# Three PSUM banks at a retention chunk's start, ten background steps to a chunk, five pumps in a pair

## The chip, the cores and the metric

The kernel runs on one core of a Trainium2 chip. The metric is the device time of one execution in microseconds (us); the time before is the median of 3 runs.

## The reference, cut to what matters

One layer of a decoder is computed for 512 prompt positions and 64 sample positions together (576 columns, kept as two halves of 288). A combined projection feeds three branches: retention, window attention and a short convolution. Each branch is projected, gated and summed; an output projection, a feed-forward network and a per-layer embedding gate follow. The retention branch works in chunks of 128 positions with a state that passes from chunk to chunk:

```python
def step(s, inp):
    qi, ki, vi = inp
    inner = jnp.einsum('bhid,bhjd->bhij', qi, ki) * dmask
    o = jnp.einsum('bhij,bhje->bhie', inner, vi) + jnp.einsum('bhid,bhde->bhie', qi * q_dec, s)
    s = s * c_dec + jnp.einsum('bhjd,bhje->bhde', ki * k_dec, vi)
    return s, o
...
o = o * lax.rsqrt(jnp.mean(o * o, axis=-1, keepdims=True) + EPS)
return jax.nn.silu(rg) * o, s
```

## The kernel before

**Matrix products.** Weights are 128x128 tiles. Every fp32 weight and activation is split into a high and a low part, and three matmuls (high-high, high-low, low-high) stand for one. `product` (L329) is twelve matmuls of 288 columns into one PSUM bank: four tiles times three parts. `pair` multiplies a 2x2 block matrix by a Strassen-like scheme in seven such products, issued in this order: b11 (bank `pa`), t3 (`pe`), t2 (`pbb`), b21 (`pa`), t1 (`pbb`), t4 (`pe`), b22 (`pbb`). Between them ScalarE copies banks (L390, L396, L400), and `done` hands out a finished quarter. In `value`, VectorE forms c22 from `pbb` (L426) after t1, and b22 then adds to that same bank; it forms c21 from `pe` (L424) after t4. `unit` (L501) is a plain product of 24 matmuls for the branch projections.

**Weights.** `step()` advances a generator that loads raw weights through SP's DMA queue, adds blocks on VectorE (L227), casts the high part on ScalarE (L256) and subtracts for the low part on VectorE (L257). Four high and four low buffers hold what is ready.

**Background work.** `pump()` runs one step of a generator, up to its next `yield`. Before, a `pair` has four pumps: after t3, after the c11 hand-out that follows b21, after t4, and at its end. Each `unit` of a branch projection has one. `ret_gen` is the first background generator. A chunk's first step transposes v (bank `pv`, L708), multiplies k by q (banks `pst[0]`, `pst[1]`, L713; each head pair uses columns 0 to 255), masks both on VectorE (L717) and transposes k into a fourth bank `pk` (L721), which VectorE scales (L723). The third step makes the chunk's output `po` (L737, L739). The fifth updates the state (L744, L751) and enters `ret_out`: ScalarE squares `po` (L681). The seventh sums the squares on TensorE (`pn`, L685) and runs `rsqrt`: VectorE transposes and adds (L548, L554), POOL raises to a power (L555), VectorE finishes (L556, L557, L560, L562), then multiplies `po` by the gate (L690) and by the result (L691). An eighth empty step follows. Called below "the chain": L685 to L691.

The conv stage is six pairs, the gate stages are four times a pair and two units, and three pairs make the attention inputs. `ret_gen` runs four chunks and then the sample part (L763 onward) across the conv stage, the conv gates and the attention inputs. `att_gen` runs under the four retention gates; `drain()` finishes what is left of it before the attention gates.

**Banks and order.** The pool `psum` has six banks, shared by `pa`, `pe`, all background banks and most unit banks; `psb` has two, for `pbb`. A tile framework sets buffers, waits and the order of each engine's instructions ahead of time; on the chip each engine works through its list in that order. The order is not strictly the program's: an instruction of a later step may stand ahead of an earlier one.

Of the kernel before, what the change touches and what calls it, by code (L numbers as in the profile page):

```python
# [84 lines left out]
def decoder_step(ctx: ExitStack, tc: tile.TileContext, xT, pT, W, consts, smalls, s0q, s0t, ckT, cv,  # L85
# [25 lines left out]
    def nm(s):  # L111
        uid[0] += 1
        return f"{s}{uid[0]}"
# [7 lines left out]
    def bgtile(dt=F32):  # L121
        return bgt.tile([P, 512], dt, tag="bgt", name=nm("bgt"))

    def bank(s="ps"):
        return psum.tile([P, 512], F32, tag="ps", name=nm(s))

    def seeded(s="pbb"):
        return psb.tile([P, 512], F32, tag="ps", name=nm(s))
# [7 lines left out]
    def halft():  # L136
        return hlf.tile([P, H], F32, tag="hlf", name=nm("hlf"))
# [158 lines left out]
    def step(n=1):  # L296
        for _ in range(n):
            next(make, None)
# [17 lines left out]
    def nextpair():  # L316
        j, kind = items[pos[0]]
        assert kind != "one"
        need(j, "t2")
        pos[0] += 1  # L320
        return made.pop(j).w

    def product(bank, w, x, start):

        (hi, lo), s = w
        for j in range(4):
            xh, xl = x(j)
            for i, (lhs, rhs) in enumerate(((hi, xh), (hi, xl), (lo, xh))):
                PE.matmul(bank[:, :H], lhsT=lhs[:, s + j, :], rhs=rhs, start=start and j == 0 and i == 0,  # L329
                          stop=j == 3 and i == 2, skip_group_check=True)  # L330
# [52 lines left out]
    def pair(X, done, first=False, **kw):  # L383


        q = Job()
        q.w, q.t = nextpair(), {}
        q.a, q.b, q.e = bank("pa"), seeded(), bank("pe")
        product(q.a, q.w["b11"], X("a11"), True)
        A.activation(q.b[:, :H], q.a[:, :H], AF.Copy, scale=-1.0)  # L390
        if first:
            product(q.a, q.w["b21"], X("a12"), False)
            done(q, "c11")
        product(q.e, q.w["t3"], X("s3"), True)
        q.es = halft()
        A.copy(out=q.es, in_=q.e[:, :H])  # L396
        step()
        pump()
        product(q.b, q.w["t2"], X("s2"), False)
        A.copy(out=q.e[:, :H], in_=q.b[:, :H])  # L400
        if not first:
            product(q.a, q.w["b21"], X("a12"), False)
            done(q, "c11")
        step()
        pump()
        product(q.b, q.w["t1"], X("s1"), False)
        done(q, "c22")
        product(q.e, q.w["t4"], X("a22"), False)
        done(q, "c21")
        step()  # L410
        pump()
        product(q.b, q.w["b22"], X("x3"), False)
        done(q, "c12")
        step()
        pump()
# [64 lines left out]
    def pump(n=1):  # L480
        for _ in range(n):
            while bg:
                try:
                    next(bg[0])
                    break
                except StopIteration:
                    bg.pop(0)
# [184 lines left out]
    for t in (0, 2):  # L672
        pair(ops, gate_r(t), t == 0)
# [3 lines left out]
    def ret_out(po, w, c0):  # L677

        ov = po[:, :4 * w]
        sq = bgtile()  # L680
        A.activation(sq[:, :4 * w], ov, AF.Square)  # L681
        yield
        yield
        pn = bank("pb")
        PE.matmul(pn[:, :4 * w], lhsT=ones_h, rhs=sq[:, :4 * w], start=True, stop=True)  # L685
        rs = bgtile()
        rsqrt(pn[:, :4 * w], 4 * w, rs[:, :4 * w], 0.5)
        t1 = bgtile()
        t1v = t1[:, :4 * w].rearrange("p (h i) -> p h i", h=4)
        V.tensor_tensor(out=t1v, in0=ov.rearrange("p (h i) -> p h i", h=4), in1=rg[:, :, c0:c0 + w], op=ALU.mult)  # L690
        V.tensor_tensor(out=ro[:, :, c0:c0 + w], in0=t1v,  # L691
                        in1=rs[:, :4 * w].rearrange("p (h i) -> p h i", h=4), op=ALU.mult)

    def hrow(h):
        return slice(64 * (h % 2), 64 * (h % 2) + 64)

    def odd(a, q):

        return a.rearrange("p (t q i) -> p t q i", t=2, q=2)[:, :, q, :]

    def ret_gen():
        vt = big.tile([P, 4, T], F32, tag="big", name="vt")
        state = None
        for c in range(4):
            cs = slice(128 * c, 128 * c + 128)
            pv = bank("pb")
            for h in range(4):
                PE.transpose(pv[:, 128 * h:128 * h + 128], rv[:, h, cs], ident)  # L708
            vc = vt[:, c, :512]
            A.copy(out=vc, in_=pv)  # L710
            pst = [bank("pb") for _ in range(2)]
            for h in range(4):
                PE.matmul(pst[h % 2][:, 128 * (h // 2):128 * (h // 2) + 128], lhsT=rk[hrow(h), h // 2, cs],  # L713
                          rhs=rq[hrow(h), h // 2, cs], start=True, stop=True)
            st = bgtile()
            for q in range(2):
                V.tensor_tensor(out=odd(st, q), in0=pst[q][:, :256].rearrange("p (t i) -> p t i", t=2),  # L717
                                in1=odd(cst[:, C_DMASK:C_DMASK + 512], q), op=ALU.mult)
            pk = bank("pb")
            for hp in range(2):  # L720
                PE.transpose(pk[:, 128 * hp:128 * hp + 128], rk[:, hp, cs], ident)  # L721
            kd = bgtile()
            V.tensor_tensor(out=kd[:, :256].rearrange("p (h d) -> p h d", h=4),  # L723
                            in0=pk[:, :256].rearrange("p (h d) -> p h d", h=4),
                            in1=cst[:, C_KDEC:C_KDEC + 4].unsqueeze(2).to_broadcast([P, 4, 64]), op=ALU.mult)
            if c:
                qd = bgtile()
                G.memset(qd, 0.0)
                for h in range(2):
                    V.tensor_tensor(out=odd(qd, h)[hrow(h)], in0=rq[hrow(h), :, cs],  # L730
                                    in1=cst[hrow(h), C_QDEC:C_QDEC + 256].rearrange("p (t i) -> p t i", t=2), op=ALU.mult)
            yield
            yield
            po = bank("pb")
            for h in range(4):
                o = po[:, 128 * h:128 * h + 128]
                PE.matmul(o, lhsT=vc[:, 128 * h:128 * h + 128], rhs=st[:, 128 * h:128 * h + 128], start=True, stop=c == 0)  # L737
                if c:
                    PE.matmul(o, lhsT=state[:, h // 2, :], rhs=qd[:, 128 * h:128 * h + 128], start=False, stop=True)  # L739
            yield  # L740
            yield
            pu = bank("pb")
            for h in range(4):
                PE.matmul(pu[hrow(h), 128 * (h // 2):128 * (h // 2) + 128], lhsT=kd[:, 64 * h:64 * h + 64],  # L744
                          rhs=vc[:, 128 * h:128 * h + 128], start=True, stop=True)
            new = mpool.tile([P, 2, P], F32, tag="rstate", name=nm("rstate"), bufs=2)
            if c == 0:
                A.copy(out=new, in_=pu[:, :256].rearrange("p (h e) -> p h e", h=2))
            else:
                for hp in range(2):  # L750
                    V.scalar_tensor_tensor(new[:, hp, :], state[:, hp, :], cst[:, C_CDEC + hp:C_CDEC + hp + 1],  # L751
                                           pu[:, 128 * hp:128 * hp + 128], op0=ALU.mult, op1=ALU.add)
            state = new
            yield from ret_out(po, 128, 128 * c)
            yield
            yield
        G.dma_start(out=o_rp, in_=state)


# [6 lines left out]
        pst = [bank("pb") for _ in range(2)]  # L766
# [16 lines left out]
        pk = bank("pb")  # L783
# [23 lines left out]
        for h in range(4):  # L807
# [13 lines left out]
            G.dma_start(out=o_rs[:, h, :], in_=s0)  # L821

    bg.append(ret_gen())


# [33 lines left out]
    def conv_pair(t):  # L859
        cc, z = [[tmpt() for _ in range(2)] for _ in range(2)]  # L860
        pair(ops, keep(cc))
        pair(ops, keep(z))
        y = []
        for m in range(2):
            y.append(tmpt())
            conv_taps(t + m, z[m], cc[m], y[m])

        def done(q, which):
            m, i = where(which)
            h = HS[i]  # L870
            v = value(q, which, q.t.setdefault(which, halft()) if i else None)
            V.tensor_tensor(out=y[m][:, h], in0=y[m][:, h], in1=v, op=ALU.mult)
            split(y[m][:, h], CH[:, t + m, h], CL[:, t + m, h])

        pair(ops, done)
# [614 lines left out]
```

## Time and profile before

| | |
|---|---|
| median of 3 runs | 987.39 us (986.63 to 988.03) |
| profiled execution, its own time | 987.22 us |
| its span in the profile | 985.4 us |
| TensorE busy / weight loads | 957.6 us (97%) / 925.0 us (94%) |
| VectorE, ScalarE, POOL busy | 712.6 us, 531.5 us, 187.1 us |
| mean granted TensorE clock | 0.994 |

The span leaves out 1.8 us around the instructions. Matmuls overlap in the pipeline, so TensorE's busy time counts a queue that is full, not work at its peak; idle times before an instruction, and what ended them, are the better guide. An instruction's wait stands in brackets behind its row in the timeline.

### The profile page before, as it was taken

Reading aid. Unit: us, or ns where it says so; the run is one execution under the profiler, and the core shown is the slowest. Engines: PE = TensorE matmul, PEld = TensorE weight load, DVE = VectorE, ACT = ScalarE, POOL = GpSimd, SP = SyncE. Lnnn points to the kernel's source line nnn. Section 1 sums busy time; section 2 is a strip of 40 time slices with the busy share of each in tenths; the row PEclk is TensorE's granted clock in tenths of the full one; section 3 lists DMA queues with packets and bytes.
Section 4 is the critical chain, followed back from the end, with each engine's and each line's share of the span. In section 5 each row is a group of like instructions: output and inputs, shape, how many; then the busy total and the mean of one; then the engine's idle time right before and its main releaser. Section 6 shows DMA issues by size and latency. Waiting matters only on the chain.

```text
span 985.4 us, 18290 instructions
## 1 busy us (share of the span) xinstructions
PE 957.6 (97%) x7081; PEld 925.0 (94%) x7081; DVE 712.6 (72%) x1308; ACT 531.5 (54%) x1051; POOL 187.1 (19%) x257
## 2 busy tenths in 40 slices
PE   9999999989989999999999999999999999999998
PEld 9999898989979888799999999999999999999897
DVE  7898789765576776577427878558847965785986
ACT  7345444433345564545436455468558845885642
POOL 0414443433324222332001100000010011000010
PEclk9999999999999999999999999999999999999999
DMA  8637565658779665688522532444486368593112
GB/s 301 168 86 199 165 138 146 163 164 220 194 218 248 143 153 153 143 226 252 187 66 71 223 108 100 155 148 145 120 199 192 110 153 222 164 356 109 65 62 79
DMA packets 65576, 160.45 MB, mean 163 GB/s; under 512 B 8089, under 2 KB 11193, under 8 KB 64241
## 3 DMA queue, kind: packets, MB, share of 16 engines
q1 hardware_dynamic: 48672, 114.75, 34.9%
q0 software_dynamic: 16672, 44.48, 21.8%
q8 instruction: 55, 0.90, 0.4%
q14 instruction: 33, 0.26, 0.1%
q10 hardware_dynamic: 144, 0.06, 0.0%
HBM read 139.17 MB, written 51.55 MB: 194 GB/s over the span
## 4 chain that ended last, share of the span: by engine, by line
PE 77%; DVE 13%; DMA 4%; ACT 2%; issue 2%; POOL 1%; SPq 0%; ACTq 0%; DVEq 0%; POOLq 0%
PE pm L501 31%; PE pbb L329 18%; PE pa L329 12%; PE pe L329 12%; DMA wst<-in_W 3%; DVE wlo L257 3%; POOL rs_b L555 1%; DVE hlf L1149 1%; DVE xl L579 1%; DVE x L1150 1%; DVE wst L227 1%; DVE s L952 1%; PE pb L964 1%; ACT whi L256 1%; DVE wlo L164 1%
## 5 line engine op out<-in xcount | busy, mean ns | idle before, releaser
L257 DVE TENSOR_TENSOR wlo<-wst,whi 128x1024 fp32r<-128x1024 f32 (+1 forms) x180 | 195.4, 1087 | 95.9 <-ACT whi L256 95.1
L256 ACT CAST whi<-wst 128x1024 fp32r<-128x1024 f32 (+1 forms) x180 | 168.3, 940 | 129.9 <-PE pe L329 29.9
L329 PE MATMUL pbb<-xs,whi 128*128 128x288 f32 x1080 | 227.1, 302 | 10.0 <-DVE akv L426 4.1
L329 PEld LDWEIGHTS pbb<-xs,whi 128*128 128x128 f32 x1080 | 174.9, 190 | 19.0 <-DVE akv L426 4.9
L329 PE MATMUL pbb<-xs,wlo 128*128 128x288 f32 x540 | 160.6, 297 | 0.0
L329 PE MATMUL pa<-fq,whi 128*128 128x288 f32 x720 | 147.7, 297 | 0.6 <-DVE fq L583 0.5
L329 PEld LDWEIGHTS pa<-fq,whi 128*128 128x128 f32 x720 | 116.0, 189 | 2.3 <-DVE fq L583 0.7
L329 PE MATMUL pa<-fq,wlo 128*128 128x288 f32 x360 | 106.8, 297 | 0.4 <-DVE wlo L257 0.4
L329 PEld LDWEIGHTS pbb<-xs,wlo 128*128 128x128 f32 x540 | 102.7, 190 | 0.0
L163 ACT CAST whi<-wst 128x1024 fp32r<-128x1024 f32 (+1 forms) x64 | 61.5, 965 | 70.9 <-PE pm L501 48.8
L501 PE MATMUL pm<-xl,whi 128*128 128x288 f32 x384 | 95.0, 299 | 1.5 <-DVE xl L579 1.4
L501 PE MATMUL pm<-xh,whi 128*128 128x288 f32 x384 | 94.9, 300 | 1.5 <-ACT xh L578 1.4
L501 PE MATMUL pm<-xh,wlo 128*128 128x288 f32 x384 | 93.5, 296 | 0.3 <-DVE wlo L164 0.3
L164 DVE TENSOR_TENSOR wlo<-wst,whi 128x1024 fp32r<-128x1024 f32 (+1 forms) x64 | 71.2, 1118 | 23.7 <-ACT whi L163 21.3
L268 POOL COPY pace<-whi 128x1 f32<-128x1 f32 x61 | 36.6, 600 | 240.8 <-ACT whi L256 190.3
L227 DVE TENSOR_TENSOR wst<-wst 128x512 f32<-128x512 f32 x90 | 61.1, 686 | 28.7 <-DMA wst<-in_W 28.0
L555 POOL TENSOR_TENSOR rs_b<-rs_a,mhalf 128x9 f32<-128x9 f32 (+2 forms) x15 | 34.8, 2322 | 222.7 <-DVE rs_a L554 222.7
L329 PE MATMUL pe<-xs,whi 128*128 128x288 f32 x360 | 73.5, 294 | 0.1
L329 PE MATMUL pe<-fq,whi 128*128 128x288 f32 x360 | 73.3, 296 | 0.0
L501 PE MATMUL pm<-fq,whi 128*128 128x288 f32 x384 | 70.4, 296 | 0.0
L329 PEld LDWEIGHTS pa<-fq,wlo 128*128 128x128 f32 x360 | 67.9, 189 | 1.9 <-DVE wlo L257 1.1
L501 PEld LDWEIGHTS pm<-xh,whi 128*128 128x128 f32 x384 | 65.7, 188 | 3.9 <-ACT xh L578 2.4
(280 smaller groups left out, 2025.6 us busy)
## 6 DMA issues: line engine op xcount, KB each, us to landing
wst<-in_W SPq DMA_DIRECT2D x86, 512.0 KB, 4.5
wst<-in_W SPq DMA_DIRECT2D x105, 256.0 KB, 3.3
ts<-in_W POOLq DMA_DIRECT2D x90, 256.0 KB, 5.7
wst<-ts SPq DMA_DIRECT2D x60, 256.0 KB, 3.3
ts<-ts POOLq DMA_DIRECT2D x30, 256.0 KB, 3.5
df<-tmp POOLq DMA_DIRECT2D x16, 288.0 KB, 5.1
x<-in_xT SPq DMA_DIRECT2D x10, 288.0 KB, 4.2
dacc<-tmp SPq DMA_DIRECT2D x8, 288.0 KB, 4.3
```

What stands on the lines that cost most here:

```text
L163: A.copy(out=hi[:, c, :], in_=st[:, c, :])
L164: V.tensor_tensor(out=lo[:, c, :], in0=st[:, c, :], in1=hi[:, c, :].bitcast(F32), op=ALU.subtract)
L227: V.tensor_tensor(out=out, in0=a, in1=b, op=ALU.add)
L256: A.copy(out=hi, in_=r[:, :n, :])
L257: V.tensor_tensor(out=lo, in0=r[:, :n, :], in1=hi.bitcast(F32), op=ALU.subtract)
L268: t = G.tensor_copy(out=pace, in_=hi[:, 0, :1].bitcast(F32))
L329: PE.matmul(bank[:, :H], lhsT=lhs[:, s + j, :], rhs=rhs, start=start and j == 0 and i == 0, stop=j == 3 and i == 2, skip_group_check=True)
L501: PE.matmul(p[:, :H], lhsT=lhs[:, kw, :], rhs=r, start=s, stop=e)
L555: G.tensor_tensor(out=b, in0=a, in1=mhalf[:, :nb], op=ALU.pow)
L579: V.scalar_tensor_tensor(lo, src, gain(gi, k), hi.bitcast(F32), op0=ALU.mult, op1=ALU.subtract)
L952: V.scalar_tensor_tensor(s[:, h, :], dist, -SLOPES[h], p[g][:, i * w:i * w + w], op0=ALU.mult, op1=ALU.add)
L964: PE.matmul(po[grow(g), :], lhsT=avt[:, 128 * chunk + 64 * g:128 * chunk + 64 * g + 64], rhs=sb[g], start=kh == 0, stop=kh == nk - 1)
```

## The change

Two places are edited. In `pair`, the second pump moves ahead of the b21 product, and the pump that stood after t4's hand-out is kept while one more is put between c22's hand-out and t4, so that a pair has five pumps instead of four. In `ret_gen`, the k transposes no longer take a bank of their own: they go to columns 256 to 511 of `pst[1]`, whose columns 0 to 255 hold scores that L717 reads. At a chunk's end there are four empty steps instead of two, so that a chunk has ten steps instead of eight. `att_gen` and the sample part of `ret_gen` keep their steps and meet more pumps.

```diff
@@ pair
         pump()
         product(q.b, q.w["t2"], X("s2"), False)
         A.copy(out=q.e[:, :H], in_=q.b[:, :H])
+        pump()
         if not first:
             product(q.a, q.w["b21"], X("a12"), False)
             done(q, "c11")
         step()
-        pump()
         product(q.b, q.w["t1"], X("s1"), False)
         done(q, "c22")
+        pump()
         product(q.e, q.w["t4"], X("a22"), False)
         done(q, "c21")
         step()
@@ ret_gen
-            pk = bank("pb")
+            pk = pst[1][:, 256:]
             for hp in range(2):
                 PE.transpose(pk[:, 128 * hp:128 * hp + 128], rk[:, hp, cs], ident)
...
             yield from ret_out(po, 128, 128 * c)
-            yield
-            yield
+            for _ in range(4):
+                yield
```

## Rows read from the trace of the kernel before

**Rows 1.** The page's first part, busy time by engine.
```profile
PE 957.6 (97%) x7081; PEld 925.0 (94%) x7081; DVE 712.6 (72%) x1308; ACT 531.5 (54%) x1051; POOL 187.1 (19%) x257
```
**Rows 2.** Waits of PE: total us, times, longest us.
```profile
PE pb L721 <- DVE bgt L690: 5.3, 2, 2.9
PE pbb L329 <- DVE akv L426: 4.1, 1, 4.1
PE pbb L329 <- DVE tmp L426: 3.5, 2, 2.9
```
**Rows 3.** Timeline of PE at the starts of chunks 1, 2, 3: start us, us.
```profile
115.26 0.71 PE L713 MATMUL pb<-rqk 64*128 64x128 f32 x8
118.39 0.69 PE L721 MATMUL pb<-cst,rqk 128*128 128x128 f32 x2 [2.42 <-DVE bgt L690]
...
150.16 0.44 PE L721 MATMUL pb<-cst,rqk 128*128 128x128 f32 x2 [2.92 <-DVE bgt L690]
...
176.57 0.71 PE L713 MATMUL pb<-rqk 64*128 64x128 f32 x8
177.31 0.44 PE L721 MATMUL pb<-cst,rqk 128*128 128x128 f32 x2
```
**Rows 4.** Windows: length, PE, PEld, DVE, ACT, POOL busy (x), PEclk, DMA share, GB/s.
```profile
118.40:121.10 2.70, 2.70 (x12) 2.70 (x13) 2.70 (x7) 0.00 (x0) 0.00 (x0) 0.50 0.65 208
...
145.20:176.30 31.10, 28.18 (x216) 26.86 (x215) 26.71 (x52) 14.62 (x27) 12.46 (x22) 1.00 0.57 153
...
209.40:213.00 3.60, 3.56 (x16) 3.56 (x17) 2.83 (x9) 2.63 (x5) 0.00 (x0) 0.58 0.00 0
...
274.30:278.00 3.70, 3.67 (x17) 3.67 (x18) 2.14 (x4) 0.96 (x2) 1.70 (x3) 0.57 0.71 229
```
**Rows 5.** Timeline of DVE, end of chunk 0 and start of chunk 1.
```profile
110.42 0.71 DVE L548 STREAM_TRANSPOSE tmp<-pb 128x512 f32<-128x512 f32 x1
...
114.89 0.17 DVE L556 SCALAR_TENSOR_TENSOR rs_d<-rs_b 128x16 f32<-128x16 f32 x1 [2.97 <-POOL rs_b L555]
...
115.31 0.69 DVE L560 SCALAR_TENSOR_TENSOR tmp<-rs_d,rs_b 128x512 f32<-128x512 f32 x1
...
117.06 0.70 DVE L562 STREAM_TRANSPOSE bgt<-tmp 128x512 f32<-128x512 f32 x1
117.68 0.65 DVE L690 TENSOR_TENSOR bgt<-pb,rg 128x512 f32<-128x512 f32 x1
...
118.91 0.68 DVE L691 TENSOR_TENSOR ro<-bgt,bgt 128x512 f32<-128x512 f32 x1
...
120.89 0.42 DVE L717 TENSOR_TENSOR bgt<-pb,cst 128x256 f32<-128x256 f32 x1
```
**Rows 6.** Timeline of DVE at the start of chunk 3.
```profile
176.82 0.18 DVE L556 SCALAR_TENSOR_TENSOR rs_d<-rs_b 128x16 f32<-128x16 f32 x1 [2.69 <-POOL rs_b L555]
...
181.84 0.41 DVE L717 TENSOR_TENSOR bgt<-pb,cst 128x256 f32<-128x256 f32 x1
```
**Rows 7.** Timeline of PE, second conv gate, with chunk 3's chain.
```profile
198.34 1.02 PE L685 MATMUL pb<-bgt,ones_h 128*128 128x512 f32 x2
198.80 0.83 PE L329 MATMUL pbb<-xs,whi 128*128 128x288 f32 x2
...
209.44 0.54 PE L329 MATMUL pbb<-xs,whi 128*128 128x288 f32 x2 [2.90 <-DVE tmp L426]
```
**Rows 8.** Timeline of DVE in the same stretch.
```profile
204.86 0.17 DVE L556 SCALAR_TENSOR_TENSOR rs_d<-rs_b 128x16 f32<-128x16 f32 x1 [3.06 <-POOL rs_b L555]
...
208.34 0.68 DVE L691 TENSOR_TENSOR ro<-bgt,bgt 128x512 f32<-128x512 f32 x1
208.94 0.45 DVE L426 TENSOR_TENSOR tmp<-hlf,pbb 128x288 f32<-128x288 f32 x1
```
**Rows 9.** The chain that ended last: start us, us, what.
```profile
106.06 1.60 PE pbb L329 x12
```
**Rows 10.** Timeline of PE, sample scores and their transposes, first retention gate.
```profile
315.31 0.29 PE L1004 MATMUL pb<-akv 64*32 64x64 f32 x8
...
321.72 0.56 PE L1017 MATMUL pb<-cst,bgt 128*128 128x128 f32 x2 [0.92 <-DVE bgt L902]
```
**Rows 11.** Timeline of DVE, first pair of the attention inputs.
```profile
271.36 0.69 DVE L227 TENSOR_TENSOR wst<-wst 128x512 f32<-128x512 f32 x1 [3.15 <-DMA wst<-in_W]
```

## The prediction

> **What bounds the kernel now.** I read the page first. TensorE is busy 97% of the span and VectorE 72% [rows 1], so a change that adds no matmuls can only win or lose what TensorE waits. The view of PE's waits then names the place: its largest entry is 5.3 us in two waits of L721, the k transposes, for L690, the multiplication that ends the chain of the chunk before [rows 2]. The transposes read only constants and k, so what they wait for is not data but a bank: `po` stays held until L690 has read it. At a chunk's start six banks are in use (`pa`, `pe`, `pv`, two `pst`, the old `po`), and `pk` is the seventh.
>
> The timeline of PE shows the price. At chunk 1 the last score matmul ends at 115.97 (115.26 + 0.71) and L721 starts at 118.39, 2.42 us idle; at chunk 2 it is 2.92 us; at chunk 3 L721 starts 0.03 us behind L713's end (177.31 against 177.28), with no wait [rows 3]. After the first of these waits the granted clock is 0.50 from 118.4 to 121.1, the 1.2 GHz level, which costs 2.7 x 0.5 = 1.35 us; after the second no fall is to be seen (1.00) [rows 4].
>
> VectorE's timeline says why L690 is late. L556 waits 2.97 us for POOL's power operation with VectorE idle, because its list is worked through in order, and L562 and L690 follow behind [rows 5]. The same wait is 2.69 and 3.06 us at the next chains that I read [rows 6, 8]. From 145.2 to 176.3 VectorE is busy 26.7 of 31.1 us [rows 4]; with two waits for POOL of about 2.8 us hardly anything is free, so its lateness has little room to be made good.
>
> The second place is the second conv gate. Chunk 3's chain starts at 198.34 (L685); b22 starts at 209.44 after 2.90 us of waiting for L426, which stands behind L691 in VectorE's list [rows 7, 8]. The clock is then 0.58 over 3.6 us, another 3.6 x 0.42 = 1.5 us [rows 4].
>
> **The change part by part.** *Bank removed.* Each chunk start asks for five of six banks beside the old `po`, so no wait for L690 is left there. Gain at chunk 1: 2.42 + 1.35 = 3.8 us; at chunk 2: 2.9 us; at chunk 3: 0. Bounds: 0, if another wait takes the place (rivals below), to 6.7 us.
>
> *Chunk of ten steps, pair of five pumps.* Two pairs had 8 pumps for 8 steps and have 10 for 10, so chunks still start after every second t3. What moves is inside: `pn` was in the third pump of the second pair, after t4; it comes in the second pump, after t2. That is three products earlier (b21, t1, t4), 3 x 1.60 = 4.8 us [rows 9]. So the chain is over well before the next chunk.
>
> *The second conv gate.* The six conv pairs now hold 30 pumps, three chunks exactly. Chunk 3 takes pumps 31 to 40, the first gate (a pair and two units) takes 31 to 37, and `pn`, the seventh step, comes in its last unit rather than after t3 of the next pair: two products earlier, 3.2 us. The wait was 2.90 us [rows 7], so it should go, with its clock: 2.9 + 1.5 = 4.4 us. Bounds: 0 to 4.4. The sample part still starts between t4 and b22 of that pair. Together up to 3.8 + 2.9 + 4.4 = 11.1 us are taken away.
>
> *What the earlier chain meets.* In chunks 0, 1 and 2 it now starts between t2 and b21, and L426 is wanted soon after. TensorE reaches b22 at the start of L685 + 0.46 (198.80 - 198.34) + three products of 1.60 = 5.3 us. On VectorE, L556 started 6.5 us after L685 (204.86 - 198.34) [rows 7, 8]. If L426 is listed behind L556, it ends at the earliest at 6.5 + 0.17 + 0.45 = 7.1 us, 1.8 us too late; behind L691, as in the second gate, it ends at 209.39 - 198.34 = 11.05 us, 5.8 us too late; ahead of L556, in the wait for POOL, it costs nothing. L426 becomes ready 3.7 us behind L685 (0.46 + 2 x 1.60), when the chain is in its first half, so I take a place one short operation past the first: 2.3 us a chunk, 6.9 us for three. Bounds 0 and 5.8 each. Behind the waiting b22 nothing but the next pair is queued on TensorE, and ScalarE's c12 copy waits with it.
>
> *Shared bank.* The transposes now follow L717 in the same bank. At chunk 1 the second L717 ends at 121.31, 5.3 us after the scores; at chunk 3 at 182.25, 5.0 us after [rows 3, 5, 6]. But four operations of the chain, L560, L562, L690 and L691 (0.69 + 0.70 + 0.65 + 0.68 = 2.7 us), stood in front of it [rows 5], and are now past. 5.0 - 2.7 leaves 2.3 us. Where b22 has already waited for VectorE, that lateness has been paid, and matmuls of t2 can be listed ahead of the transposes; I take 0 beside the 2.3 us above, bounds 0 and 2.3 for each of three starts.
>
> *Attention and the rest.* The sample scores come in `att_gen`'s third step, its sample transposes (L1017) in the fifth. Before, b22 and a 24-matmul unit half-work lay between (4.8 us); after, t4 and b22 (3.2 us). L1017 already waits 0.92 us for the softmax [rows 10]; it waits 1.6 us longer. Bounds 0 and 3. All 28 steps now fit in the retention gates' 28 pumps (24 before), so the drain's bunched last four steps are spread; more of the others stand one product apart, and I count these two against each other, 0, within 1 either way. The added pump calls issue no instruction of their own, and no DMA is added; the four state loads of the sample part come closer together in SP's queue, which I cost at 0 because TensorE showed no wait for them, at most one wait like the 2.9 us above if that cover goes.
>
> Sum: -11.1 + 6.9 + 1.6 = -2.6 us. The profiled execution took 987.22 us, so 984.6; its distance to the median, 987.39, is 0.17, which gives 984.8, and I say 984.7.
>
> **The rivals.** *A, slower: the wait goes to b22.* The mechanism is the second gate's, at three pairs: L426 stands behind the chain in VectorE's list. For it speaks that this is just what rows 7 and 8 show; against it, that L426 is ready earlier in the chain than there. It decides from (11.1 - 1.6) / 3 = 3.2 us a chunk. Halfway between 2.3 and 5.8, 4.0 us, with one fall of the clock of 1.4 us, gives -11.1 + 12.0 + 1.6 + 1.4 = +3.9: 991.3. The whole 5.8 gives 995.
>
> *B, slower: the shared bank.* The transposes wait for L717 at each chunk start, on top of b22's wait: 3 x 2.3 = 6.9 us more, -2.6 + 6.9 = +4.3: 991.7. For it speaks that L717 came 5 us late at chunk 3, where TensorE took no notice because only `po` needed it; against it, that the chain no longer stands in front.
> The Trainium skill, page "PSUM — Partial Sum Buffer", section "PSUM bank collisions raise a hardware error", has TensorE's writes kept apart from VectorE's reads by bank, also where they touch different columns. By that rule the transposes cannot start before L717 is through; no row here shows two such accesses in one bank, so the trace neither bears it out nor speaks against it.
>
> *C, much faster: nothing comes back.* L426 is listed ahead of L556 and the transposes wait nowhere: -11.1 + 1.6 = -9.5, 977.9. Chunk 2's chain speaks for it, whose lateness cost nothing at chunk 3 [rows 3, 6]; VectorE's full stretch [rows 4] speaks against it.
>
> *D, no change: a later wait swallows it.* In the attention inputs L227 waits 3.15 us for a weight load and L426 behind it; TensorE waits 4.1 us, and the clock is 0.57 after that [rows 2, 4, 11]. If that load's time is set by DMA and not by TensorE's progress, arriving 2.6 us earlier only lengthens the wait: 987.3.
>
> **How the numbers follow.** Forecast (-1 to -5.5 us, so 982 to 986.5) 0.36, A 0.18, B 0.12, C 0.12, D 0.22. A measurement of this kernel tells about 0.2%, 2 us, from no change. Faster by more: 0.30 of the forecast, C, and 0.02 of D, 0.44. Within: 0.06 of the forecast, 0.18 of D, 0.03 of A, 0.27. Slower: the rest of A, B and D, 0.29. For the range 979.0 to 992.0 I leave out most of C and the upper parts of A and B, 2 in 10.
>
> **What would show it.** Right: no wait of L721 for L690; L685 right behind t2 in chunks 0 to 2; no wait of b22 in the second conv gate, and clock 1.00 there; a wait of b22 for L426 of 1 to 3 us in the second, fourth and sixth conv pair; L1017's wait at 2.5 us. Wrong: waits of b22 above 3.2 us (A), L721 waiting for L717 (B), neither (C), or a longer wait for the weight load near 270 us (D).

## The result, and the profile after

The changed kernel took 994.38 us (median of 12 runs, 990.29 to 997.44), the kernel before 986.76 us beside it (12 runs, 980.99 to 992.00): ratio 1.0079, 95% interval 1.0063 to 1.0095. It is slower by 7.6 us where 2.6 us less was forecast, and it lies above the range. Behind the edit of `pair`, lines of the kernel after are one higher than those of before: the b22 product's bank is freed by L427, the chain is L686 to L692, the k transposes are L722, the mask L718.

First the page's busy times, then PE's waits (engine, line, what it waited for: total us, times, longest us):

```profile
PE 960.7 (97%) x7081; PEld 930.0 (94%) x7081; DVE 713.4 (72%) x1308; ACT 532.2 (54%) x1051; POOL 196.0 (20%) x257
```
```profile
PE pbb L329 <- DVE tmp L427: 11.2, 3, 6.1
PE pbb L329 <- DVE hlf L427: 3.4, 1, 3.4
PE pbb L329 <- DVE aq L427: 2.3, 1, 2.3
...
PE pbb L329 <- DVE akv L427: 1.7, 1, 1.7
```

The span grew by 8.3 us (985.4 to 993.7). TensorE's busy time is 3.1 us more for the same 7081 matmuls [rows 1], so some of them ran at a lower clock; the other 5.2 us are idle. The 5.3 us of the k transposes [rows 2] are gone from the list. In their place, L427 holds up b22 in three places more than before: three waits of `tmp` and one of `hlf`, where the kernel before had one of 2.90 us [rows 7]. The timeline of PE has the four places: the second, fourth and sixth conv pair, and the second conv gate.

```profile
104.61 1.02 PE L686 MATMUL pb<-bgt,ones_h 128*128 128x512 f32 x2
...
117.87 0.85 PE L329 MATMUL pbb<-xs,whi 128*128 128x288 f32 x2 [6.12 <-DVE tmp L427]
...
148.99 0.54 PE L329 MATMUL pbb<-xs,whi 128*128 128x288 f32 x2 [2.02 <-DVE tmp L427]
...
181.65 0.85 PE L329 MATMUL pbb<-xs,whi 128*128 128x288 f32 x2 [3.43 <-DVE hlf L427]
...
221.82 0.85 PE L329 MATMUL pbb<-xs,whi 128*128 128x288 f32 x2 [3.04 <-DVE tmp L427]
```

The windows right behind these four waits, and one in the attention inputs (length, PE, PEld, DVE, ACT, POOL busy, PEclk, DMA share, GB/s), show a mean granted clock between 0.53 and 0.72, that is for a part of each window at the 1.2 GHz level:

```profile
117.90:124.60 6.70, 6.70 (x38) 6.52 (x38) 5.38 (x10) 3.33 (x7) 3.01 (x5) 0.65 0.28 75
148.90:152.40 3.50, 3.41 (x17) 3.41 (x18) 3.50 (x8) 0.40 (x1) 0.06 (x1) 0.65 0.86 170
181.70:188.50 6.80, 6.80 (x32) 6.80 (x33) 4.72 (x10) 2.41 (x5) 2.56 (x4) 0.58 0.24 77
221.80:225.20 3.40, 3.38 (x14) 3.39 (x15) 2.81 (x9) 2.18 (x5) 0.00 (x0) 0.53 0.11 26
302.00:305.40 3.40, 3.40 (x19) 3.40 (x20) 3.40 (x7) 3.15 (x6) 0.32 (x1) 0.72 1.00 268
```

VectorE's timeline at chunk 0 says why L427 is late:

```profile
108.61 0.69 DVE L227 TENSOR_TENSOR wst<-wst 128x512 f32<-128x512 f32 x1 [3.17 <-DMA wst<-in_W]
109.22 0.71 DVE L549 STREAM_TRANSPOSE tmp<-pb 128x512 f32<-128x512 f32 x1
...
114.02 0.18 DVE L557 SCALAR_TENSOR_TENSOR rs_d<-rs_b 128x16 f32<-128x16 f32 x1 [2.83 <-POOL rs_b L556]
...
116.18 0.70 DVE L563 STREAM_TRANSPOSE bgt<-tmp 128x512 f32<-128x512 f32 x1
116.81 0.65 DVE L691 TENSOR_TENSOR bgt<-pb,rg 128x512 f32<-128x512 f32 x1
117.38 0.44 DVE L427 TENSOR_TENSOR tmp<-hlf,pbb 128x288 f32<-128x288 f32 x1
```

The sum of squares starts at 104.61 where it started at 109.09 before, 4.5 us earlier. Its first VectorE step, the transpose, starts at 109.22 against 110.42 [rows 5], only 1.2 us earlier, because an L227 that waits for a weight load stands in front of it. Then VectorE waits for GpSimd's power as before, and L427 comes behind L691, with only L692 of the chain behind it. In chunks 1 and 2 L427 stands much earlier in VectorE's list, behind L558, the second operation after the power:

```profile
147.18 0.17 DVE L557 SCALAR_TENSOR_TENSOR rs_d<-rs_b 128x16 f32<-128x16 f32 x1 [3.05 <-POOL rs_b L556]
...
148.49 0.44 DVE L427 TENSOR_TENSOR tmp<-hlf,pbb 128x288 f32<-128x288 f32 x1
...
180.60 0.17 DVE L557 SCALAR_TENSOR_TENSOR rs_d<-rs_b 128x16 f32<-128x16 f32 x1 [3.50 <-POOL rs_b L556]
...
181.15 0.45 DVE L427 TENSOR_TENSOR hlf<-hlf,pbb 128x288 f32<-128x288 f32 x1
```

### The profile page after: what moved, and what is told of

Read it like the earlier page. It is cut to its first block, busy times and chain, and to the rows that moved or that the text cites. A ratio compares the mean times of both kernels' runs of the same rounds, so it can differ in the third digit from the quotient of the medians.

```text
span 993.7 us, 18290 instructions
## 1 busy us (share of the span) xinstructions
PE 960.7 (97%) x7081; PEld 930.0 (94%) x7081; DVE 713.4 (72%) x1308; ACT 532.2 (54%) x1051; POOL 196.0 (20%) x257
## 4 chain that ended last, share of the span: by engine, by line
PE 80%; DVE 11%; DMA 3%; issue 2%; POOL 2%; ACT 2%; SPq 0%; POOLq 0%; DVEq 0%; ACTq 0%
PE pm L502 32%; PE pbb L329 19%; PE pa L329 12%; PE pe L329 12%; DVE wlo L257 2%; DMA wst<-in_W 2%; POOL rs_b L556 2%; DVE hlf L1150 1%; DVE xl L580 1%; DVE x L1151 1%; PE pb L965 1%; DVE wst L227 1%; PE pb L948 1%; DMA out_o_rs<-bgt 1%; DMA x<-in_xT 1%
## 5 line engine op out<-in xcount | busy, mean ns | idle before, releaser
L257 DVE TENSOR_TENSOR wlo<-wst,whi 128x1024 fp32r<-128x1024 f32 (+1 forms) x180 | 195.5, 1087 | 104.3 <-ACT whi L256 102.7
L329 PE MATMUL pa<-fq,whi 128*128 128x288 f32 x720 | 153.9, 305 | 0.6 <-DVE fq L584 0.5
L329 PEld LDWEIGHTS pa<-fq,whi 128*128 128x128 f32 x720 | 118.6, 192 | 7.6 <-issue 5.7
L268 POOL COPY pace<-whi 128x1 f32<-128x1 f32 x61 | 45.4, 745 | 225.8 <-ACT whi L256 167.6
L227 DVE TENSOR_TENSOR wst<-wst 128x512 f32<-128x512 f32 x90 | 61.1, 686 | 22.2 <-DMA wst<-in_W 21.4
```

The lines of the kernel that those rows point to most:

```text
L227: V.tensor_tensor(out=out, in0=a, in1=b, op=ALU.add)
L257: V.tensor_tensor(out=lo, in0=r[:, :n, :], in1=hi.bitcast(F32), op=ALU.subtract)
L268: t = G.tensor_copy(out=pace, in_=hi[:, 0, :1].bitcast(F32))
```

## Experiments

Ratios are to the kernel before on the same chip, with 95% intervals. Its medians there were 986.14 us for `bank_only`, `pumps_only`, `squares_after_t4` and `no_power`; 986.23 for `squares_after_c22`, `before_no_power`, `early_gain` and `early_gain_t4`; 986.53 for the three with the power passed.

**Each half of the change alone.** `bank_only` has the new bank and the old pumps; `pumps_only` the new pumps and steps, and a bank of its own.

```
bank_only:   -  pk = bank("pb")             (kernel before)
             +  pk = pst[1][:, 256:]
pumps_only:  -  pk = pst[1][:, 256:]        (kernel after)
             +  pk = bank("pb")
```

> The kernel before with one edit: the k transposes go into the upper half of the second score bank; four pumps and eight steps as before. Theory (the loss comes from the chain's new place, between t2 and b21, where VectorE's wait for POOL stands ahead of c22): the two waits of the transposes for the end of the chain (5.3 us) go, nothing comes instead, 981 to 985 us. Rival S (the shared bank costs): transposes wait for the mask, 990 to 995 us.

> The changed kernel with the k transposes in a bank of their own again; five pumps and ten steps stay. Theory: the waits of b22 for c22 in the second, fourth and sixth conv pair stay (11.6 us in the changed kernel) and so do the stretches at half clock, 992 to 997 us. Rival S: the loss is gone, 984 to 988 us.

`bank_only`: 990.55 us, 1.0039 (1.0024 to 1.0054). `pumps_only`: 991.18 us, 1.0047 (1.0029 to 1.0066). Each half is slower alone, and the two excesses together, 0.86%, are about that of the whole, 0.79%. The expectation of 981 to 985 us for the bank was a miss: its rival S, the transposes waiting for the mask, came true. `pumps_only` has the expected waits and lies just under the expected 992 to 997 us. PE's waits in `bank_only`, and its timeline at the three chunk starts, with the mask that ends the first wait:

```profile
PE pb L721 <- DVE bgt L717: 8.3, 3, 3.0
```
```profile
120.29 0.41 DVE L717 TENSOR_TENSOR bgt<-pb,cst 128x256 f32<-128x256 f32 x1
120.76 0.44 PE L721 MATMUL pb<-cst,rqk 128*128 128x128 f32 x2 [2.95 <-DVE bgt L717]
...
150.28 0.69 PE L721 MATMUL pb<-cst,rqk 128*128 128x128 f32 x2 [2.86 <-DVE bgt L717]
...
182.61 0.44 PE L721 MATMUL pb<-cst,rqk 128*128 128x128 f32 x2 [2.44 <-DVE bgt L717]
```

The two waits for L690, 5.3 us [rows 2], have become three for the mask, 8.3 us. The mask stands behind the whole chain in VectorE's list, so a bank that waits for it frees later than `po`, which waited for L690 inside the chain. The profiled execution of `bank_only` took 987.45 us, 3.1 less than the median, so this trace shows where the time goes and not all of it. In `pumps_only` the longest wait of b22 is 6.0 us, with no shared bank to help it.

**Where in the pair the sum of squares stands.** Two versions of the kernel after move it later, behind t4 and behind c22.

```
squares_after_t4:    -  yield; yield                ahead of pn
                     +  for _ in range(4): yield    (and 2 trailing steps)
squares_after_c22:   +  for _ in range(3): yield    (and 3 trailing steps)
```

> The changed kernel with the chain two steps later: four empty steps instead of two ahead of the sum of squares, and two instead of four at the chunk's end. Five pumps, ten steps and the shared bank stay; the chain starts behind c22 and c21. Theory: b22 waits under 0.5 us in the conv pairs, clock 1.00 there, 981 to 986 us. Rival P (denser background steps as such cost, wherever the chain stands): 992 to 997 us.

> The kernel after with the sum of squares one pump later (after t1 and c22, ahead of t4) and three trailing steps. Theory: c22 is then ahead of the chain in VectorE's list, so b22's waits (11.6 us in three) go, and c21 behind it has the whole of b22 as cover: 983 to 987 us, unless the shared bank still waits for the mask as in the version after t4 (988). Rival: the planned list puts the chain before c22 again and the time stays at 992 to 995 us.

988.08 us, 1.0014 (1.0000 to 1.0029), and 989.16 us, 1.0023 (1.0005 to 1.0041). PE's waits of the version behind c22:

```profile
PE pb L722 <- DVE bgt L718: 6.2, 3, 2.4
PE pbb L329 <- DVE tmp L427: 5.5, 2, 3.2
```

Two of b22's four waits go, and three for the mask come, as in `bank_only`; behind t4 the mask's three are 7.4 us. Both are faster than the kernel after, but not as fast as expected: b22 still waits in the second pair, 2.27 us here and 3.08 us behind t4. That wait is not the chain's. In VectorE's timeline of the version behind c22, L427 comes before the chain's first operation there (L549, at 112.19), behind an L227 that waits for its weight load:

```profile
108.88 1.29 DVE L227 TENSOR_TENSOR wst<-wst 128x512 f32<-128x512 f32 x2 [3.24 <-DMA wst<-in_W]
...
111.83 0.45 DVE L427 TENSOR_TENSOR tmp<-hlf,pbb 128x288 f32<-128x288 f32 x1
```

So the second pair has a second cause of lateness beside the chain. VectorE's wait for a weight load between 100 and 112 us is 2.7 to 4.6 us in the eight traces of kernels with five pumps, and 0.4 to 2.4 us in the five with four. No run changes the loads alone, so why they come later is open.

**Without the power.** In the retention output of both kernels a VectorE multiply takes the place of GpSimd's power.

```
-  G.tensor_tensor(out=b, in0=a, in1=mhalf[:, :nb], op=ALU.pow)
+  V.tensor_tensor(out=b, in0=a, in1=mhalf[:, :nb], op=ALU.mult)    (retention output only)
```

> The changed kernel with POOL's power operation in the retention output replaced by a multiplication on VectorE, so that the retention output is not normalised (this part of the computation is changed); all else stays. Theory: VectorE's waits of 2.8 to 3.5 us for POOL in the chain go, b22's waits for c22 fall below 1.5 us each, 980 to 987 us. If the chain's own work and not the wait for POOL holds c22 back, b22 still waits 2 us or more three times, and the time stays at 990 to 995 us.

> The kernel before, with GpSimd's power in the retention output replaced by a VectorE multiply (the retention output is then not normalised). Theory: in the kernel before, the three waits that come from a chain (two of the k transposes for the last line of the chain's bank, one of the second conv gate for c22) are all that GpSimd's power costs, 8.2 us of waits and 2.8 us of half clock: 10 to 11 us less, 976 to 978 us. If the same list without the power is better in the kernel after (974.3) than here, the moved pumps do have a worth of their own, 2 to 3 us, which the power hides. Rival: VectorE's list is late for its DMA waits in any case, then only 2 to 4 us go.

Kernel after: 974.31 us, 0.9873 (0.9849 to 0.9896). Kernel before: 973.38 us, 0.9874 (0.9853 to 0.9894). The two kernels are then the same within what can be told, and both are faster than was expected. The power costs the kernel before 12.9 us (986.23 - 973.38), more than the 10 to 11 that its visible waits and clock had given, and the kernel after 20.1 (994.38 - 974.31, not measured side by side). The difference of the two, 7.2 us, is about all that the change lost. That the moved pumps have a worth of 2 to 3 us hidden under the power was refuted. What stays in the kernel after is one line of PE's timeline in the second pair:

```profile
112.13 0.83 PE L329 MATMUL pbb<-xs,whi 128*128 128x288 f32 x2 [3.09 <-DVE tmp L427]
```

In VectorE's timeline of this version an L227 waits 2.88 us for its weight load, until 106.89, ahead of L549 at 107.50. So of the 6.12 us about half is the power and half what stands in VectorE's list around the weight load. That the two kernels are equal although this wait stays goes with the retention gates, which five pumps shorten (see Attention below).

**The bank freed early.** The multiplication by the gate (L690), which is all that holds `po`, needs no power; here it is issued ahead of the inverse root, in the kernel before, and in `pumps_only` with the sum of squares behind t4.

```
   A.activation(sq[:, :4 * w], ov, AF.Square)
+  V.tensor_tensor(out=t1v, in0=ov..., in1=rg[...], op=ALU.mult)
   ...
   rsqrt(pn[:, :4 * w], 4 * w, rs[:, :4 * w], 0.5)
-  V.tensor_tensor(out=t1v, in0=ov..., in1=rg[...], op=ALU.mult)
```

> The kernel before, with the multiply of the output bank by the gate moved ahead of the inverse root, so that the bank the k transposes wait for is read before GpSimd's power is waited for. Theory: TensorE's lateness is paid at the next thing that it needs from behind the power. With the bank free early that is the mask behind it in VectorE's list, as in the kernel with the shared bank alone: waits of about 3 us at the k transposes go, but they come back at the scores' readers or at b22, 986 to 991 us. Rival: the mask is needed only by the output product two pumps later, so the two waits and their half clock go whole: 980 to 982 us.

> The kernel after with a bank of its own for the k transposes, the gate multiply ahead of the inverse root, and the sum of squares issued two pumps later (after t4), so that neither c22, nor the bank, nor the mask's sharing stands behind the power. Theory: what is left behind the power is c21 and the mask, which TensorE needs late: no wait over 1.5 us in the first two conv pairs, 977 to 982 us. Rival: the mask and the k decay are late for the output product of the next chunk or c21 for its reader, and the time stays at 986 to 989 us.

984.96 us, 0.9980 (0.9963 to 0.9997), and 985.75 us, 0.9998 (0.9982 to 1.0014). The transposes' waits are gone in both, and the time hardly moves. PE's waits of the first:

```profile
PE pbb L329 <- DVE tmp L426: 5.5, 4, 2.5
PE pb L739 <- DVE bgt L730: 2.9, 1, 2.9
```

In the first the output product (L739) now waits 2.9 us for the decayed q (L730), which is later still in VectorE's list. The theory that TensorE's lateness is only passed on held for its mechanism; the time, 984.96 us, lies between its 986 to 991 and the rival's 980 to 982, a gain of 0.2%. The hope of 977 to 982 us for the second, on which I had taken c21 and the mask as the only things left behind the power, did not hold: there too the output product waits for the decayed q, 4.5 us in three waits of a profiled execution of 981.52 us, and the median is next to the rival's 986 to 989.

**VectorE given work while the power runs.** All of the computation is kept. The multiplication by the gate is early, and everything that needs the power is issued in the next chunk, with its output product, and held in VectorE's list behind the latest c22 or c21.

```
 rsqrt:    G.tensor_tensor(out=b, ..., op=ALU.pow)
+          def finish(): the four VectorE operations behind the power
 ret_out:
+          def finish():
+              with tc.issue_after(latest[0].ins):   # c21 or c22
+                  second()                          # the four operations
+              V.tensor_tensor(out=ro[...], in0=t1v, in1=rs[...], op=ALU.mult)
+          pending.append(finish)
 ret_gen:  the output product of the next chunk
+          flush()                                   # runs what is pending
```

> The kernel before, all of its computation kept, with the gate multiply early and the second half of the chain (everything that needs GpSimd's power) issued behind c22 and c21 of the next pair, so that VectorE has other work while the power runs. Theory: what is lost is VectorE's 3 us of idling behind each of four powers; without the power altogether 13 us went (973.4), so most of that goes here: no wait of VectorE for the power over 0.5 us, no wait of TensorE for the chain, 974 to 978 us. Rival: the late second half (2.8 us of VectorE per chunk) now stands in front of other results that TensorE wants, and the time stays at 981 to 985 us, as with the early multiply alone.

> The same edit in the kernel after with a bank of its own for the k transposes (pumps and trailing steps as changed). Theory: the moved pumps by themselves neither cost nor bring anything once the power is passed: b22's three waits in the first two... conv pairs go, 974 to 979 us, within 3 us of the kernel before with the same edit. Rival: the earlier sum of squares still puts c22 behind part of the chain and b22 waits 2 us or more three times, 984 to 990 us.

> The same edit in the kernel after as it is, with the shared bank. Theory: with VectorE no longer late at the chunk's start the mask ends in time, and sharing the bank costs the mask's own latency at most, under 1 us at each of three starts: within 3 us of the version with a bank of its own. Rival: the transposes wait for the mask 2 us or more at each start whatever VectorE does before it: 6 us or more above it.

In the kernel before: 974.92 us, 0.9869 (0.9850 to 0.9889). With the changed pumps: 975.81, 0.9888 (0.9868 to 0.9907). With the shared bank too: 976.66, 0.9899 (0.9879 to 0.9920). All three beat both kernels, and they are too close to be told apart. With the changed pumps one of b22's three waits stays, 2.24 us in the second pair, behind the weight load as above. The page's busy line, VectorE's waits and VectorE's timeline of the first:

```profile
PE 954.2 (98%) x7081; PEld 920.6 (95%) x7081; DVE 711.8 (73%) x1308; ACT 531.7 (55%) x1051; POOL 190.0 (20%) x257
```
```profile
DVE rs_d L559 <- POOL rs_b L557: 16.1, 9, 2.0
```
```profile
112.50 0.16 DVE L556 TENSOR_SCALAR rs_a<-tmp 128x16 f32<-128x16 f32 x1
112.57 0.22 DVE L863 TENSOR_TENSOR ubuf<-tmp,tmp 128x64 f32<-128x64 f32 x1
112.75 1.23 DVE L257 TENSOR_TENSOR wlo<-wst,whi 128x1024 fp32r<-128x1024 f32 x1
...
117.72 0.74 DVE L739 TENSOR_TENSOR bgt<-pb,cst 128x256 f32<-128x256 f32 x2
...
125.39 0.45 DVE L426 TENSOR_TENSOR hlf<-pe,hlf 128x288 f32<-128x288 f32 x1
125.75 0.16 DVE L559 SCALAR_TENSOR_TENSOR rs_d<-rs_b 128x16 f32<-128x16 f32 x1
```

For comparison, the same group in the kernel before:

```profile
DVE rs_d L556 <- POOL rs_b L555: 27.6, 13, 3.1
```

Four of the 13 waits for POOL are gone, 11.5 us of VectorE's time (27.6 - 16.1), and the kernel is 11.6 us shorter (986.53 - 974.92). That the two numbers agree is no proof by itself: the profiled executions differ by 13.5 us, 10.1 of it TensorE's idle time and 3.4 its busy time. The mask is multiplied at 117.72, ahead of the operation that needs the power, which comes at 125.75 without a wait. TensorE's idle time is 17.7 us (971.9 - 954.2) against 27.8 before [rows 1]. With VectorE on time the shared bank shows no wait for the mask at all in PE's list: in these runs sharing cost something only where the mask was late.

## Why the prediction was wrong

**The bound** was read rightly: VectorE's list, worked through in order, is late by GpSimd's power, and TensorE's waits follow from that. `power_passed` and the two kernels without the power show it. What it left out is the weight load ahead of the second pair's c22. One reading was off without changing the sum: of the 4.4 us that VectorE is free from 145.2 to 176.3 [rows 4] it gave two waits of 2.8 us to POOL, but these end at 146.18 and 176.82, so only 1.0 + 2.2 us of them lie inside.

**The bank removed** went as predicted at TensorE: no wait of L722, and the 2.42 + 1.35 and 2.9 us of chunks 1 and 2 are gone. But a wait removed there makes VectorE no earlier.

**The step that failed is "what the earlier chain meets"**, the 6.9 us for three. It measured 18.0 us: 11.6 of waits (6.12, 2.02 and 3.43) and 6.4 of clock. The clock is the larger part of the miss. The prediction counted the fall of the clock behind the waits that it took away (1.35 and 1.5 us) and put it at nothing, without a reason, behind the waits that it brought; in the windows behind the three it cost 6.7 x 0.35 + 3.5 x 0.35 + 6.8 x 0.42 = 6.4 us.

The other part is the size of the waits. I took a place for L426 (now L427) one short operation past the first of the chain's second half, 2.3 us a chunk. In chunks 1 and 2 that was nearly its place, and the waits, 2.02 and 3.43 us, are near the forecast. In chunk 0 it stood behind the gate multiply (L691, which is L690 before), one line of the chain earlier than in the second gate [rows 8]. Yet the wait, 6.12 us, is above the bound of 5.8 that the second gate had given, because VectorE reached the chain's first operation 4.6 us behind L686 (109.22 - 104.61), held by the weight load. L427 ended 13.2 us behind L686 (117.82 - 104.61), and TensorE reached b22 7.1 us behind it and not 5.3.

So chunk 0 is rival A (chance 0.18), with a weight load on top, and chunks 1 and 2 are close to the forecast's own case. That A's 991.3 to 995 us holds the measured 994.38 is partly luck: its 4.0 us a chunk is close to the mean wait, 3.9, but it had 1.4 us for the clock and still counted the second gate's 4.4 us as gained.

**"The chain is over well before the next chunk"** went wrong on the way. I moved the chain with its matmul, 4.8 us; TensorE's part moved 4.5, VectorE's 1.2, held by a weight load's wait.

**The second conv gate's 4.4 us** did not come, for the same reason: VectorE was held by a weight load. Its timeline there:

```profile
208.70 1.42 DVE L227 TENSOR_TENSOR wst<-wst 128x512 f32<-128x512 f32 x2 [3.61 <-DMA wst<-in_W]
...
210.76 0.71 DVE L549 STREAM_TRANSPOSE tmp<-pb 128x512 f32<-128x512 f32 x1
...
216.10 0.17 DVE L557 SCALAR_TENSOR_TENSOR rs_d<-rs_b 128x16 f32<-128x16 f32 x1 [2.83 <-POOL rs_b L556]
...
221.31 0.45 DVE L427 TENSOR_TENSOR tmp<-hlf,pbb 128x288 f32<-128x288 f32 x1
```

L686 is at 207.41, so L557 is 8.7 us behind it, against 6.5 before, and L427 still stands behind the whole chain, with an L257 of 1.22 us more before it; b22 waits 3.04 us where it waited 2.90 [rows 7], and the clock costs 3.4 x 0.47 = 1.6 us more as before. The term is +0.2, not -4.4.

**Shared bank.** In the changed kernel's trace it cost no wait, as predicted; that this is because b22 had already waited was not tested by itself. Yet the kernel after came out 0.3% slower than `pumps_only`, which differs only in this bank (1.0079 against 1.0047, not measured side by side, with intervals that just touch). No wait on PE's list accounts for that, and the profiled execution of `pumps_only`, 994.82 us, is its slowest, so the traces do not settle it. `bank_only` shows the 2.3 us bound of rival B to be nearly right where b22 has not: 2.95, 2.86 and 2.44. There the program's own waits hold the transposes behind the mask. The Trainium skill, "PSUM — Partial Sum Buffer", section "PSUM bank collisions raise a hardware error", wants two such accesses to one bank kept apart. The trace agrees in so far as L721 starts at 120.76, behind the end of the second mask at 120.70 (120.29 + 0.41). What the chip would do without these waits was not tried.

**Attention** was +1.6. PE's timeline at the sample scores and the second sample transposes:

```profile
326.50 0.29 PE L1005 MATMUL pb<-akv 64*32 64x64 f32 x8
...
333.12 0.56 PE L1018 MATMUL pb<-cst,bgt 128*128 128x128 f32 x2
```

From the one to the other it is 6.6 us (333.12 - 326.50) against 6.4 [rows 10], with no wait for the softmax: +0.2, not +1.6. The retention gates as a whole went the other way. These are PE's rows of their first product and of the first unit product in the second attention gate, in the kernel before and then after; all background work of the attention lies between:

```profile
303.56 0.43 PE L329 MATMUL pa<-fq,whi 128*128 128x288 f32 x2
...
437.72 0.43 PE L501 MATMUL pm<-ah,whi 128*128 128x288 f32 x2
```
```profile
316.33 0.43 PE L329 MATMUL pa<-fq,whi 128*128 128x288 f32 x2
...
446.06 0.43 PE L502 MATMUL pm<-ah,whi 128*128 128x288 f32 x2
```

That is 134.16 us before and 129.73 after, 4.4 us less. In the traces of all eight kernels with five pumps the same stretch takes 129.7 to 131.1 us, in the five with four pumps 132.5 to 134.2. So the denser pumps help here, where the prediction had them cost 1.6 us. It fits the spread of the drain's steps, which I had set at 0; that was not tested by itself.

**Rival D** was partly real. TensorE's wait for L427 at the first pair of the attention inputs fell from 4.1 to 1.7 us [rows 2], where D has it grow, and the last thing that VectorE waits for ahead of L427 is there no longer a weight load but the store of a sample state (L810, 1.75 us). Another wait of 2.3 us, behind an L227 that waits 3.56 us for its weight load, appeared in the next pair, with a fall of the clock to 0.72. With the clocks, (1.7 + 2.3 + 3.4 x 0.28) - (4.1 + 1.6) = -0.7 us; the whole stage took 44.5 us against 44.1, +0.5.

By the waits and clocks, the stages up to the attention inputs should be -6.7 + 18.0 + 0.2 = +11.5 us later; TensorE starts the attention inputs at 271.81 where it started at 259.50, +12.3, so 0.8 us stay unassigned. With +0.5 in the attention inputs and -4.4 in the retention gates that is +8.4, and the two profiled spans differ by 8.3.

## What to carry to other kernels

Where an engine works its list in order and waits for another in the middle of it, ask which results stand behind that wait, and not which of them TensorE happens to wait for now: in these runs, freeing a bank or moving a matmul mostly chose who pays. Put other work of the same engine between the request and the use of its answer; here that, together with the early gate multiply, was worth 1.3% (the early multiply alone 0.2%), and every move of the waits changed the time by between +0.8% and -0.2%. When a step is moved earlier, move it on each engine by that engine's own list, and price each new wait with the clock behind it.

## What the runs showed of the hardware that was not expected

The length of a wait did not tell what the clock would do behind it: after 2.92 us at chunk 2 of the kernel before the granted clock stayed at 1.00 [rows 3, 4]; after 2.02 us in the kernel after it was 0.65 over the next 3.5 us. In `bank_only` it was 1.00 over the 3.5 us behind the waits of 2.95 and 2.44 us, and 0.51 behind that of 2.86. After 6.12 us it was 0.65 over 6.7 us, so its cost there, 2.35 us, is more than a third of the wait's own.

GpSimd's power grows with the columns: groups of POOL in the kernel after (busy us, mean ns) give 2.10 us for 9 columns and 3.13 us for 16, by these two widths about 0.15 us a column ((3126 - 2102) / 7); the kernel before has 2.10 and 3.04.

```profile
L556 POOL TENSOR_TENSOR rs_b<-rs_a,mhalf 128x9 f32<-128x9 f32 x10 | 21.0, 2102 | 214.8 <-DVE rs_a L555 214.8
...
L556 POOL TENSOR_TENSOR rs_b<-rs_a,mhalf 128x16 f32<-128x16 f32 x4 | 12.5, 3126 | 12.3 <-DVE rs_a L555 12.3
```
